# A two-layer transformer block on one core: the tiles that TensorE reads, all at one remainder of 512 bytes

## The chip, the core and the metric

The kernel runs on one core of a Trainium2 chip. A core has a matrix engine (TensorE, PE in the profile; PEld is its loading of weights), a vector engine (DVE), an activation engine (ACT), a general engine (POOL), an engine that issues transfers (SP), and 16 DMA engines. SBUF is the working memory, 128 partitions wide; PSUM takes the results of the matrix engine. The metric is the device time of one execution in microseconds (us).

A matmul on TensorE has two operands in SBUF. The *stationary* one, here up to 128 x 128 numbers, is loaded ahead as weights, by an instruction of its own. The *moving* one is then streamed through, here up to 512 columns. While one matmul streams its moving operand, the weights of the next are loaded, so there are two reads of SBUF at a time.

## The reference

`x` is 512 x 1024 in float32. Two layers, each of them:

```python
x = layer_norm(ALPHA * x + 0.5 * swiglu(x, ffn1_w1, ffn1_w2))   # (silu(x @ w1a) * (x @ w1b)) @ w2, width 2816
x = layer_norm(ALPHA * x + token_mix(x))
x = layer_norm(ALPHA * x + 0.5 * swiglu(x, ffn2_w1, ffn2_w2))
```

`token_mix` projects `x` with `w_in` (3616 columns) and runs three attentions side by side, each with 8 heads of 64: one over compressed, selected and windowed keys (`Nsa`), one over a window of 128 with sinks (`Swa`), and one with forget gates (`Fox`). Each result passes through a matrix of its own and a sigmoid gate of `x`, the three are added and multiplied with `w_out`.

## The kernel before, in words

**Numbers.** Every float32 matrix product of the dense parts is made of three products of rounded parts: a value is split into `hi` (rounded) and `lo` (the rest), and `hi*hi + lo*hi + hi*lo` is summed in PSUM. So nearly all matmuls come in threes. `xh` and `xl` hold the transposed input of a stage split in this way, 1024 x 512. Weights arrive by DMA as `raw` tiles of 512 KB; ACT makes `hi` of them (L140) and DVE makes `lo` (L141), in `wsplit` (L129).

**Two kinds of product.** In `mm3` (L155, matmuls L161 to L163; L158 and L159 for a narrow one) the weights are stationary and `xh`/`xl` move, 512 columns. In `mm_rows` (L169, matmuls L174 to L176) the activations are stationary, 128 columns at a time, and the weights `hi`/`lo` move, 512 columns. `value_rows` (L335, matmuls L345 to L347) does the latter with `xh`/`xl` as the stationary part.

**A feed-forward** (`ffn`, L271). `staged` (L255) computes the first four column blocks in halves of 256 moving columns, while the last tiles of the stage before are being transposed into `xh`/`xl` (`LN.second`, L211, transposes at L218). Then for f = 2 to 21 the gate block `pg` and the up block `pu` are computed, 24 matmuls each; their product goes as two rounded parts into `ha` (f below 18) and `hb` (the last 4). `rows_ln` (L223) then multiplies with `w2`: the main part runs over the 18 blocks of `ha`, 24 matmuls for each, into 8 accumulators `acc`; the last four, from `hb`, are done one row block at a time, so that each row block's layer norm (`LN.first`, L191) can start while PE goes on with the next. Before these last four, `ha`'s place is released and the pool `nx` is opened on it, into which the first weights of the next stage are loaded.

**The layer norm** of a row block: DVE adds the residual `xa` (L198), ACT squares (L201), POOL takes the power -1/2 in two small steps (L203, L204), DVE scales and shifts (L202, L207). The sums and the scale of a row are kept in `st`, 8 numbers a partition, one tile for each of the four row blocks.

**The mix** (`mix`, L352). `value_rows` first, from weights in `nx`. Then projections are cut into small pieces (`chunk`, three matmuls for a piece `pj`) which `step` (L995) puts between the attention's scores (`sS`, `sF`, `sN`, `sC`), transposes of the probabilities (`ptS`, `ptF`, `ptN`, `ptC`, against the identity `ident`) and products with the values (`po`). Afterwards the gates (`gate`), the three branch matrices (`brp`, with `oh`/`ol` moving) and `w_out` (`acc` from `mh`/`ml`) follow, and a layer norm.

**What sets the order.** The order on PE and POOL, and on SP at the beginning, is the order of the code; on the other engines a scheduler orders the instructions at build time.

**Where tiles lie.** SBUF is given out by pools. A pool opened later lies above (with `side="right"`, below the top), and within a pool tiles follow each other. Sizes in bytes per partition, addresses counted from the partition's beginning, before the change:

| tiles | pool | first address | remainder of 512 |
|---|---|---|---|
| `ident` | `const` | 16,512 | 128 |
| `xh`, `xl` | `xtp` | 19,776 | 320 |
| `raw`, `hi`, `lo` | `wt` (some `hi`, `lo` in `wx`, 89,408) | 52,544 | 320 |
| `hb`, and in the mix `mh`, `ml` | `fb`, `tl` | 105,792 | 320 |
| `st`, 4 x 32 bytes | `lnp` | 138,560 | |
| `ha`, 73,728 bytes | `fa` | 138,688 | 448 |
| `hi`, `lo` of a next stage | `nx` | 138,688 | 448 |
| `v4`, then `gt` of 384 bytes | `at` | 89,408 | 320 |
| `ks`, `qs`, `vt`, `p`, `pc` and others of the attention | `at` | 97,984 | 192 |
| `kc2`, `vbd` | `at` | 195,392 | 320 |
| `oh`, `ol` | `ohp` | 146,752 | 320 |
| `xa`, four residual tiles | `xap` | 212,960 | 480 |

`at.tile` without a tag gives a tile its place at its first call; `kc2` and `vbd` are first asked for in `conv2` (L575), after the small tiles of the first attention. `need` (L977) holds an `Nsa` unit back until `kc2` and `vbd` exist on `m`.

Of the kernel before, what the change touches and what calls it, by code (L numbers as in the profile page):

```python
# [9 lines left out]
F32 = mybir.dt.float32  # L10
F32R = mybir.dt.float32r
# [7 lines left out]
P = 128  # L19
S, D, F = 512, 1024, 2816  # L20
KD, KF, NB = D // P, F // P, S // P
H, DH, NSLOT = 8, 64, 32
# [42 lines left out]
def body(tc, a, out, depth=DEPTH):  # L65
# [3 lines left out]
    def pool(name, bufs=1, side=None, **kw):  # L69
        return tc.alloc_tile_pool(name=name, bufs=bufs, side=side, **kw)  # L70

    const = pool("const")
# [8 lines left out]
    def ps(tag=None, name="ps", shape=(P, 512)):  # L81
        if tag is None:
            tag = PS_ALL[ring[0] % 8]
            ring[0] += 1
        return psp.tile(list(shape), F32, name=name, tag=tag, bufs=PS_TAGS[tag])
# [15 lines left out]
    foxb = const.tile([P, depth, H], F32, name="foxb")  # L101
    bgate = const.tile([P, depth, 3, KD], F32, name="bgate")
    peT = const.tile([P, depth, 2, 32], F32, name="peT")

    xh = xtp.tile([P, KD, S], F32R, name="xh")
    xl = xtp.tile([P, KD, S], F32R, name="xl")
# [48 lines left out]
    def mm3(o, w, k, vh, vl, first, last):  # L155
        hi, lo = w
        if lo is None:
            nc.tensor.matmul(o[0:64], hi[:, k, 0:64], vh, start=first, stop=False)  # L158
            nc.tensor.matmul(o[0:64], hi[:, k, 0:64], vl, start=False, stop=last)  # L159
            return  # L160
        nc.tensor.matmul(o, hi[:, k], vh, start=first, stop=False)  # L161
        nc.tensor.matmul(o, hi[:, k], vl, start=False, stop=False)  # L162
        nc.tensor.matmul(o, lo[:, k], vh, start=False, stop=last)  # L163
# [15 lines left out]
    class LN:  # L179
# [10 lines left out]

        def first(self, acc, tb, tpl):  # L191
            x = self.xa[tb]
            st = self.pl.tile([P, 8], F32, name="st", bufs=4)
            junk = tpl.tile([P, D], BF, name="junk", bufs=2)
            u = tpl.tile([P, D], F32, name="u", bufs=2)
            hs = [slice(0, 512), slice(512, 1024)]
            for hf, c in enumerate(hs):
                nc.vector.scalar_tensor_tensor(x[:, c], acc[hf], self.scale, x[:, c], op0=OP.mult, op1=OP.add,  # L198
                                               accum_out=st[:, hf:hf + 1])
            nc.vector.tensor_scalar(st[:, 2:3], st[:, 0:1], st[:, 1:2], -1.0 / D, op0=OP.add, op1=OP.mult)  # L200
            nc.scalar.activation(junk, x, AF.Square, bias=st[:, 2:3], accum_out=st[:, 3:4])  # L201
            nc.vector.scalar_tensor_tensor(u, x, st[:, 2:3], self.G, op0=OP.add, op1=OP.mult)  # L202
            nc.gpsimd.tensor_scalar(st[:, 4:5], st[:, 3:4], 1.0 / D, EPS / ALPHA ** 2, op0=OP.mult, op1=OP.add)  # L203
            nc.gpsimd.tensor_tensor(st[:, 5:6], st[:, 4:5], mhalf, op=OP.pow)  # L204
            for c in hs:
                y = u if self.last else x
                nc.vector.scalar_tensor_tensor(y[:, c], u[:, c], st[:, 5:6], self.B[:, c], op0=OP.mult, op1=OP.add)  # L207
                if self.last:
                    nc.sync.dma_start(out[tb * P:(tb + 1) * P, c], y[:, c])
# [38 lines left out]

    def alloc_xa():
        p = pool("xap", side="right", reuse_waits="tile")  # L250
        return p, [p.tile([P, D], F32, name=f"xa{t}") for t in range(NB)]

    halves = [slice(0, 256), slice(256, 512)]

# [13 lines left out]
    def ffn_first(w1):  # L268
        return [wcols(w1, c) for c in (0, F, P, F + P)]
# [82 lines left out]
    def mix(l, wts, pend, done_ffn, xap, xa, nxt):  # L352
        m = K()
# [13 lines left out]
        at = pool("at", reuse_waits="tile")  # L367
# [1 line left out]
        for tb in range(NB):  # L369
            nc.scalar.activation(v4[:, tb], pts[tb], AF.Copy)  # L370
        m.vb, m.vs, m.vw = (v4[:, :, j] for j in range(3))
        gt = at.tile([P, NB, 24], F32, name="gt")
        tabs = {}

        def toep(i, mm):
# [198 lines left out]

        def conv2(c):  # L575

            m.kc2 = at.tile([P, 2, 2, NSLOT], F32R, name="kc2")
            m.vbd = at.tile([P, 2, P], F32, name="vbd")
            nc.gpsimd.memset(m.vbd, 0.0)
            p = ps("tp", "kv", (P, 3, 64))  # L580
            for f in range(2):
                nc.tensor.matmul(p[:, 0], c.wk[:, f].rearrange("p r d -> p (r d)"), c.gk[:, f], start=f == 0, stop=f == 1)
            for g in range(2):
                for f in range(2):
                    nc.tensor.matmul(p[0:64, 1 + g], c.gv[:, f, g].rearrange("p r n -> p (r n)"), c.wv[:, f],
                                     start=f == 0, stop=f == 1)
            hi, lo = m.kc2[:, :, 0], m.kc2[:, :, 1]
            pk = p[:, 0].rearrange("p (g n) -> p g n", g=2)
            nc.scalar.activation(hi, pk, AF.Copy, scale=0.5)
            nc.vector.scalar_tensor_tensor(lo, pk, 0.5, hi.bitcast(F32), op0=OP.mult, op1=OP.subtract)  # L590
            for r in range(2):
                o = slice(32 * r, 32 * r + 32)
                nc.scalar.activation(m.vbd[o, :, 64 * r:64 * r + 64], p[o, 1:3], AF.Copy, scale=0.5)
# [357 lines left out]
        fill.append(tr)  # L951
        chunk(CQA, set_q(m.qa, 0))
        fill.insert(len(fill) - 2, lambda: conv2(cv))
        fox_chunks(1)
        chunk(CQA + P, set_q(m.qa, 1))
# [21 lines left out]
        def need(u):  # L977
            if u.br == 1:
                return u.m in m.qb and hasattr(m, "kb")
            if u.br == 2:  # L980
                return u.m in m.qc and u.m in m.kc and u.m in m.vc and u.m in m.nck
            return u.m in m.qa and hasattr(m, "vbd") and hasattr(m, "kc2")

        batches = []
        for i in range(4):
# [9 lines left out]
        def step(cur, prev, n):  # L995


            for u in cur:
                while not need(u):
                    pump(1)  # L1000
                    n -= 1
# [85 lines left out]
        for d in range(KD):  # L1087
            g_t = gates0 if d == 0 else g_1 if d == 1 else gates(d)
            for br in (1, 2, 0):
# [3 lines left out]
                p = ps(name="brp")  # L1093
                for k in range(4):
                    mm3(p, w, k0 + k, oh[br][k], ol[br][k], k == 0, k == 3)
                t = g_t[br]
# [5 lines left out]
        ohp.release()  # L1102
        op.release()
        xap2, xa2 = alloc_xa()
        lnp = pool("lnp2", reuse_waits="tile")
        ln = LN(lnp, 1, l, xa2, 0.5)
# [12 lines left out]

    more_open()  # L1120
    xap, xa = alloc_xa()
    first_w = a["ffn1_w1"][0]
    pre = []
# [84 lines left out]
    for l in range(depth):  # L1208
        fin = l == depth - 1
        wts, pend, done = ffn(l, a["ffn1_w1"][l], a["ffn1_w2"][l], 0, xa, wts, pend, done, False, lambda: mix_first(l))  # L1210
        wts, pend, done, xap, xa = mix(l, wts, pend, done, xap, xa, lambda: ffn_first(a["ffn2_w1"][l]))
        wts, pend, done = ffn(l, a["ffn2_w1"][l], a["ffn2_w2"][l], 2, xa, wts, pend, done, fin,
                              lambda: None if fin else ffn_first(a["ffn1_w1"][l + 1]))
# [30 lines left out]
```

## Time and profile before

| | us |
|---|---|
| median of 3 runs | 2569.75 (2567.87 to 2570.13) |
| profiled execution, its own time | 2569.09 |
| its span, first to last instruction | 2567.4 |
| first feed-forward: `pg`/`pu`, from 41.3; `ha`, from 260.7 | |
| first mix: `vr` from 384.9, attention from 429.9, gates and branches from 709.6, `w_out` from 878.4 | |
| second feed-forward: `pg` from 948.3, `ha` from 1165.9 | |
| third feed-forward: `pg` from 1315.0, `ha` from 1532.7 | |
| second mix: `vr` from 1656.8 | |
| fourth feed-forward: `pg` from 2219.8, `ha` from 2437.4 | |

The granted TensorE clock was 0.998 of full speed over the span. In the rows of the profile, `L174 PE MATMUL acc<-hi,ha 128*128 128x512 f32 x576 | 227.3, 395 | 0.0` reads: line, engine, operation, result from moving and stationary tile, stationary size, moving size, count, then busy us in total, mean ns of one, and the engine's idle us just before. In a view of one tile the numbers after the count are shortest, median and longest duration in ns, then the first and the last start in us. In a timeline the first number is the start in us and the second the duration. Durations of matmuls overlap: the next starts before the last has ended.

### The profile page before, as it was taken

To read this page: it belongs to the slowest core of one execution; us is meant where nothing else is said; L and a number is where in the kernel's file an instruction comes from. 1 tells how busy PE (TensorE), PEld (TensorE's weight loads), DVE (VectorE), ACT (ScalarE), POOL (GpSimd) and SP (SyncE) were. 2 spreads that over 40 slices of the span, in tenths; PEclk is the share of its full clock that TensorE was granted. 3 is DMA by queue.
4 is the path that set the end of the run, shared out by engine and by line. 5 is a ranking of instruction groups with operands and counts; after the bars stand their busy time and mean duration, and the time that the engine had idled before them with its cause. 6 is when DMAs were issued, how large, how long until landed. Compare 5 with 4: busy or idle time off the path is not lost.

```text
span 2567.4 us, 34066 instructions
## 1 busy us (share of the span) xinstructions
PE 2545.5 (99%) x13099; PEld 2110.8 (82%) x13099; DVE 1214.1 (47%) x2617; ACT 927.4 (36%) x1895; POOL 187.6 (7%) x371
## 2 busy tenths in 40 slices
PE   9999999999999999999999999999999999999998
PEld 8888887788888888888888888877888888888887
DVE  4433245577654363332344432555776534544323
ACT  3222133476642332222232221345766323322211
POOL 0000000133300000000000000101332000000000
PEclk9999999999999999999999999999999999999999
DMA  6333234623143333333433333435321434233331
GB/s 213 111 98 99 95 96 122 181 79 83 50 140 102 120 100 98 99 99 91 115 91 94 95 98 99 116 117 155 95 75 42 146 101 148 81 93 98 99 94 63
DMA packets 375172, 268.98 MB, mean 105 GB/s; under 512 B 17385, under 2 KB 351273, under 8 KB 375009
## 3 DMA queue, kind: packets, MB, share of 16 engines
q1 hardware_dynamic: 373856, 262.61, 35.1%
q0 software_dynamic: 1152, 4.19, 0.4%
q8 instruction: 103, 1.69, 0.3%
q14 instruction: 61, 0.49, 0.1%
HBM read 247.83 MB, written 9.49 MB: 100 GB/s over the span
## 4 chain that ended last, share of the span: by engine, by line
PE 97%; DVE 1%; ACT 1%; DMA 1%; issue 0%; POOL 0%; DVEq 0%; POOLq 0%; SPq 0%; ACTq 0%
PE acc L176 7%; PE acc L174 7%; PE acc L175 7%; PE pg L161 6%; PE pg L162 6%; PE pg L163 6%; PE pu L161 6%; PE pu L163 6%; PE pu L162 6%; PE pj L161 5%; PE pj L163 5%; PE pj L162 5%; PE gate L161 3%; PE gate L162 3%; PE gate L163 3%; PE brp L162 2%
## 5 line engine op out<-in xcount | busy, mean ns | idle before, releaser
L141 DVE TENSOR_TENSOR lo<-raw,hi 128x1024 fp32r<-128x1024 f32 (+2 forms) x414 | 490.3, 1188 | 852.0 <-ACT hi L140 851.3
L140 ACT ACTIVATE hi<-raw 128x1024 fp32r<-128x1024 f32 (+2 forms) x414 | 424.4, 1031 | 1236.0 <-issue 702.2
L161 PE MATMUL pj<-xh,hi 128*128 128x512 f32 (+1 forms) x720 | 267.1, 371 | 1.5 <-ACT vt L448 1.4
L163 PE MATMUL pj<-xh,lo 128*128 128x512 f32 (+1 forms) x720 | 255.0, 354 | 0.2 <-DVE lo L141 0.2
L162 PE MATMUL pj<-xl,hi 128*128 128x512 f32 (+1 forms) x720 | 254.6, 354 | 0.0
L161 PE MATMUL pg<-xh,hi 128*128 128x512 f32 x640 | 249.9, 390 | 0.0
L162 PE MATMUL pg<-xl,hi 128*128 128x512 f32 x640 | 249.7, 390 | 0.0
L163 PE MATMUL pg<-xh,lo 128*128 128x512 f32 x640 | 249.5, 390 | 0.0
L163 PE MATMUL pu<-xh,lo 128*128 128x512 f32 x640 | 249.0, 389 | 0.0
L161 PE MATMUL pu<-xh,hi 128*128 128x512 f32 x640 | 249.0, 389 | 0.0
L162 PE MATMUL pu<-xl,hi 128*128 128x512 f32 x640 | 249.0, 389 | 0.0
L174 PE MATMUL acc<-hi,ha 128*128 128x512 f32 x576 | 227.3, 395 | 0.0
L175 PE MATMUL acc<-hi,ha 128*128 128x512 f32 x576 | 227.3, 395 | 0.0
L176 PE MATMUL acc<-lo,ha 128*128 128x512 f32 x576 | 227.2, 395 | 0.0
L286 DVE TENSOR_TENSOR t<-t,pu 128x512 f32<-128x512 f32 x80 | 55.0, 687 | 216.6 <-PE pu L163 216.6
L163 PEld LDWEIGHTS pj<-xh,lo 128*128 128x128 f32 x720 | 135.8, 189 | 20.1 <-DVE lo L141 0.4
L161 PEld LDWEIGHTS pj<-xh,hi 128*128 128x128 f32 x720 | 136.3, 189 | 17.6 <-issue 3.1
L203 POOL TENSOR_SCALAR st<-st 128x1 f32<-128x1 f32 x24 | 8.5, 355 | 1891.8 <-ACT junk L201 1891.8
L162 PEld LDWEIGHTS pj<-xl,hi 128*128 128x128 f32 x720 | 136.5, 190 | 11.4
L163 PEld LDWEIGHTS pg<-xh,lo 128*128 128x128 f32 x640 | 120.5, 188 | 25.2
L161 PEld LDWEIGHTS pg<-xh,hi 128*128 128x128 f32 x640 | 120.6, 188 | 25.0
L162 PEld LDWEIGHTS pg<-xl,hi 128*128 128x128 f32 x640 | 120.6, 188 | 24.8
(245 smaller groups left out, 4323.6 us busy)
## 6 DMA issues: line engine op xcount, KB each, us to landing
raw<-in_ffn_w_dram SPq DMA_DIRECT2D x264, 512.0 KB, 3.8
raw<-in_w_in_dram SPq DMA_DIRECT2D x56, 512.0 KB, 3.8
raw<-in_w_gate_dram SPq DMA_DIRECT2D x48, 512.0 KB, 4.2
ks<-hl SPq DMA_DIRECT2D x96, 128.0 KB, 2.4
raw<-in_w_out_dram SPq DMA_DIRECT2D x16, 512.0 KB, 3.6
tab<-bvec SPq DMA_DIRECT2D x16, 256.0 KB, 3.9
x_sp<-xa POOLq DMA_DIRECT2D x8, 512.0 KB, 6.7
cw<-in_cmp_k_w_dram SPq DMA_DIRECT2D x32, 128.0 KB, 3.5
```

What stands on the lines that cost most here:

```text
L140: nc.scalar.activation(hi[:, c], raw[:, c], AF.Copy)
L141: nc.vector.tensor_tensor(lo[:, c], raw[:, c], hi[:, c].bitcast(F32), op=OP.subtract)
L161: nc.tensor.matmul(o, hi[:, k], vh, start=first, stop=False)
L162: nc.tensor.matmul(o, hi[:, k], vl, start=False, stop=False)
L163: nc.tensor.matmul(o, lo[:, k], vh, start=False, stop=last)
L174: nc.tensor.matmul(o, sh(k)[:, t], hi[:, c], start=k == 0, stop=False)
L175: nc.tensor.matmul(o, sl(k)[:, t], hi[:, c], start=False, stop=False)
L176: nc.tensor.matmul(o, sh(k)[:, t], lo[:, c], start=False, stop=k == nk - 1)
L203: nc.gpsimd.tensor_scalar(st[:, 4:5], st[:, 3:4], 1.0 / D, EPS / ALPHA ** 2, op0=OP.mult, op1=OP.add)
L286: nc.vector.tensor_tensor(t, t, pu, op=OP.mult)
```

## The change

The four `st` tiles become `stats` in the pool `const`, with a `pad` of 48 numbers behind them (4 x 32 + 192 = 320 bytes), so that `xh` and all that follows starts at remainder 128, as `ident` does, and no small tile stands between `lnp` and `ha` or `nx`. All layer norms now share these four tiles. `xa` gets a pad of 88 numbers (352 bytes) above it and moves to 128 too. `gt` is 512 bytes instead of 384, of which 384 are used. `kc2` and `vbd` get their place right behind `gt`; since they then exist from the beginning of the mix, `need` looks at a new mark, `m.c2`, which `conv2` sets. After it every tile that TensorE reads, moving or stationary, starts at remainder 128 of 512.

```diff
@@ body
     peT = const.tile([P, depth, 2, 32], F32, name="peT")
+    stats = [const.tile([P, 8], F32, name=f"st{i}") for i in range(NB)]
+    const.tile([P, 48], F32, name="pad")
@@ LN.first
-            st = self.pl.tile([P, 8], F32, name="st", bufs=4)
+            st = stats[tb]
@@ alloc_xa
-        return p, [p.tile([P, D], F32, name=f"xa{t}") for t in range(NB)]
+        xa = [p.tile([P, D], F32, name=f"xa{t}") for t in range(NB)]
+        p.tile([P, 88], F32, name="pad")
+        return p, xa
@@ mix
-        gt = at.tile([P, NB, 24], F32, name="gt")
+        gt = at.tile([P, NB, 32], F32, name="gt")[:, :, 0:24]
+        m.kc2 = at.tile([P, 2, 2, NSLOT], F32R, name="kc2")
+        m.vbd = at.tile([P, 2, P], F32, name="vbd")
@@ conv2
-            m.kc2 = at.tile([P, 2, 2, NSLOT], F32R, name="kc2")
-            m.vbd = at.tile([P, 2, P], F32, name="vbd")
             nc.gpsimd.memset(m.vbd, 0.0)
...
+            m.c2 = True
@@ need
-            return u.m in m.qa and hasattr(m, "vbd") and hasattr(m, "kc2")
+            return u.m in m.qa and hasattr(m, "c2")
```

## The prediction

> **What bounds the kernel now.** I read the engine totals and the chain first.
>
> ```profile
> PE 2545.5 (99%) x13099; PEld 2110.8 (82%) x13099; DVE 1214.1 (47%) x2617; ACT 927.4 (36%) x1895; POOL 187.6 (7%) x371
> ...
> PE 97%; DVE 1%; ACT 1%; DMA 1%; issue 0%; POOL 0%; DVEq 0%; POOLq 0%; SPq 0%; ACTq 0%
> ```
>
> TensorE (PE) is busy in 99% of the span and holds 97% of the chain. So the time is the number of matmuls times the spacing of their starts, and only two things can shorten it: fewer matmuls or a closer spacing. A matmul's duration is no spacing, because neighbours overlap, but a change in duration hints at one. The groups kept apart by shape, all with 512 moving columns:
>
> ```profile
> L161 PE MATMUL pg<-xh,hi 128*128 128x512 f32 x640 | 249.9, 390 | 0.0
> ...
> L174 PE MATMUL acc<-hi,ha 128*128 128x512 f32 x576 | 227.3, 395 | 0.0
> ...
> L161 PE MATMUL brp<-oh,hi 128*128 128x512 f32 x192 | 74.7, 389 | 0.0
> ...
> L175 PE MATMUL acc<-hi,hb 128*128 128x512 f32 x128 | 49.8, 389 | 0.0
> ...
> L346 PE MATMUL vr<-hi,xl 128*128 128x512 f32 x64 | 25.2, 394 | 0.0
> ```
>
> The same shape takes 389 to 390 ns in one set of groups and 394 to 395 ns in another. The spacing comes from first and last starts in the tile views of `ha` and `pu` (inside the first feed-forward) and, for `hb`, from the timeline:
>
> ```profile
> L174 PE MATMUL acc<-hi,ha x144: 390/393/404, 260.7 to 360.4; 128*128 128x512 f32 x144
> L176 PE MATMUL acc<-lo,ha x144: 390/393/404, 261.2 to 360.9; 128*128 128x512 f32 x144
>   ACT hi L140: 72.2, 16
> ...
> L161 PE MATMUL pu<-xh,hi x160: 389/389/389, 48.6 to 260.1; 128*128 128x512 f32 x160
> L163 PE MATMUL pu<-xh,lo x160: 389/389/396, 49.0 to 260.5; 128*128 128x512 f32 x160
> ...
> 362.75 0.39 PE L175 MATMUL acc<-hi,hb 128*128 128x512 f32 x1
> ...
> 366.83 0.39 PE L175 MATMUL acc<-hi,hb 128*128 128x512 f32 x1
> ```
>
> `ha`: 3 x 144 = 432 matmuls, 431 steps from 260.7 to 360.9 us, 232.5 ns a step. `pu` alternates with `pg` in blocks of 24: 20 x 48 - 24 = 936 matmuls, 935 steps from 48.6 to 260.5, 226.6 ns. `hb`: 18 steps in 4.08 us, 226.7 ns. So `ha` pays 5.8 ns a matmul. `hb` and `ha` run the same three lines with the same kind of moving tile; they differ only in where the stationary tile lies. The third `ha` row is from the list of who waited: ACT waited 72.2 us, in 16 waits, for these matmuls, so the weights are ready ahead of PE and a faster PE finds them.
>
> Where do the tiles lie? Tiles of a pool follow each other in SBUF, in bytes per partition. `xh`, `xl`, the pool of `hi`/`lo`, `hb`, `mh`, `ml` and `oh`/`ol` start at remainder 320 of 512. The four statistics tiles of the layer norm (32 bytes each) stand in the pool below `ha`, and push `ha` and the pool `nx` to 448. The slow groups are those in which a moving row at one remainder is read while the next weights are loaded from the other: `ha` (moving 320, stationary 448) and `vr` (448, 320). Each fast group has one remainder for both. Address height is no explanation: `oh` moves from bytes 146,752 to 195,904, as high as `ha`, at 389 ns.
>
> **The change part by part.** It changes no arithmetic, no instruction count on PE and no order: on all five engines the instructions stand in the same order before and after (only `gt` is written as 4 x 24 instead of 96 elements). What changes is addresses, and then waits that go with addresses.
>
> (a) `ha` gets remainder 128 like all others: 4 feed-forwards x 432 = 1728 matmuls x 5.8 ns = 10.0 us off. All of it lies on PE, so all is span.
>
> (b) `vr`: 64 x 3 = 192 matmuls. Their durations are `ha`'s (394), so I take 5.7 ns: 1.1 us off.
>
> (c) The token mix. There the attention tiles stand at 192 (`gt` of 384 bytes pushed them), the identity at 128 and the projections at 320.
>
> ```profile
> L161 PE MATMUL pj<-xh,hi 128*128 128x512 f32 x464 | 193.8, 418 | 1.4 <-ACT vt L448 1.4
> L163 PE MATMUL pj<-xh,lo 128*128 128x512 f32 x464 | 182.3, 393 | 0.0
> L162 PE MATMUL pj<-xl,hi 128*128 128x512 f32 x464 | 181.9, 392 | 0.0
> ...
> 599.80 0.39 PE L161 MATMUL pj<-xh,hi 128*128 128x512 f32 x1
> 600.04 0.40 PE L162 MATMUL pj<-xl,hi 128*128 128x512 f32 x1
> 600.27 0.40 PE L163 MATMUL pj<-xh,lo 128*128 128x512 f32 x1
> 600.51 0.39 PE L807 MATMUL ptN<-ident,p 128*128 128x128 f32 x2
> ...
> 601.43 0.39 PE L161 MATMUL pj<-xh,hi 128*128 128x512 f32 x1
> 601.65 0.39 PE L162 MATMUL pj<-xl,hi 128*128 128x512 f32 x1
> ```
>
> At 600.27 a projection matmul runs while the weights of a transpose (`p`, other remainder) load: 240 ns to the next start, against 220 to 230 where projections follow each other (601.43 to 601.65). But 599.80 to 600.04 is 240 ns too, and there both remainders are equal: the projection has just followed attention work, and what it loses then need not be a matter of remainders. L162 never stands next to an attention weight and still has 392 ns. So the bounds are 0 and the whole excess over 389: (393 - 389) + (392 - 389) ns x 464 = 3.2 us on two lines, and some 5 us with a like share for L161 (an estimate from the same rows). I take 1.2 us off, about two thirds of L163's 4 ns x 464 = 1.9 us, because only that line is followed by weights at another remainder.
>
> (d) Matmuls with 256 moving columns (`staged`). Here the trace speaks against the change:
>
> ```profile
> 32.37 0.28 PE L163 MATMUL pj<-xh,lo 128*128 128x256 f32 x1
> ...
> 34.77 0.28 PE L162 MATMUL pj<-xl,hi 128*128 128x256 f32 x1
> ...
> 937.72 0.28 PE L162 MATMUL pj<-xl,hi 128*128 128x256 f32 x1
> ...
> 940.34 0.28 PE L163 MATMUL pj<-xh,lo 128*128 128x256 f32 x1
> ```
>
> In the first stage both tiles are at 320: 20 steps in 2.40 us, 120.0 ns. At 937 the weights come from `nx` at 448: 22 steps in 2.62 us, 119.1 ns. Equal remainders cost 0.9 ns here. Three stages move over: 3 x 192 = 576 matmuls, 0.5 us on.
>
> (e) Short matmuls of the mix.
>
> ```profile
> L807 PE MATMUL ptN<-ident,p 128*128 128x128 f32 x320 | 48.2, 273 | 3.9 <-DVE pc L393 3.0 <-ACT p L395 0.9
> L826 PE MATMUL po<-p,v 128*64 128x128 f32 x640 | 40.4, 273 | 0.0
> ```
>
> Transposes and the products with V have never had equal remainders, so there is no row. With the kinds left out here (L218, L706, L655, L713, L663, L820) they are some 2,100 records. Nearest is (d), also with a short stream: +0.9 ns at one end, and the same 0.9 ns as a gain at the other, so 1.9 us either way. I take 0.6 us on, nearer to the cost because (d) is the nearest row.
>
> (f) Waits. Moved addresses change which earlier tile's readers a new tile waits for; all of these are readers of an earlier stage, long done. Two edits leave a wait where none was: the statistics tiles are now shared by all layer norms, so POOL's write at L204 waits for DVE's reads of the layer norm before, and `kc2` and `vbd` get space at the beginning of the mix. The former stands in the tail of the program:
>
> ```profile
> 2559.35 0.39 PE L176 MATMUL acc<-lo,hb 128*128 128x512 f32 x1
> ...
> 2562.15 0.19 POOL L203 TENSOR_SCALAR st<-st 128x1 f32<-128x1 f32 x1 [4.62 <-ACT junk L201]
> 2562.42 0.55 POOL L204 TENSOR_TENSOR st<-st,mhalf 128x1 f32<-128x1 f32 x1
> ```
>
> The DVE reads waited for are those of the layer norm before, a whole feed-forward earlier, so the wait is met on arrival. Behind it in POOL's queue stands nothing, but DVE's L207 and the last store wait for its result. Bound: 0 to one more small POOL step, 0.2 us. I take 0. `kc2`, `vbd`: 0, because their old neighbours were read for the last time a stage earlier.
>
> Sum: -10.0 - 1.1 - 1.2 + 0.5 + 0.6 = -11.2 us. From the profiled execution's own 2569.09 us that gives 2557.9. That execution lies 0.7 us under the median shown, 2569.75; I say **2558**.
>
> **The rivals.**
>
> *Nothing changes* (2569). The two reads do not disturb each other, and the 5.8 ns come from something else that `ha` and `vr` share, for instance that their upper tiles lie in the pools opened last, at byte 138,688 and above. For it: only three remainders and few pairs occur. Against it: `oh` is as high and fast, and in `vr` the high tile moves while in `ha` it is stationary. The Trainium skill's page "SBUF — State Buffer", in its sections "SBUF: two separate sides" and "A bandwidth-pool intuition that's wrong (but worth ruling out)", speaks for this rival: TensorE has ports of its own and waits on nobody, and a second, independent read port serves weight loads. By that page nothing is to be had and the sum is 0; the trace's 232.5 beside 226.7 ns for one shape does not agree with two reads that never touch.
>
> *Slower: 128 is not 320.* All clean equal pairs of the trace are at 320. Should the remainder itself count, with 128 a bad one for streams of 512, every such matmul pays d ns over 226.7. Those equal now are `pg`, `pu`, `gate`, `brp`, `hb`, `mh`/`ml` and `pj`, 7,488; with `ha` and `vr` 9,408. Change: 9,408 x d - 1,920 x 5.7 ns, which is slower by over 5 us from d = 1.7 ns; at `ha`'s full 5.7 it is +42.7, 2612 us. For it: no pair at 128 has been seen. Against it: both mixed pairs, 320/448 and 448/320, cost the same, so the difference decides.
>
> *The mix gives more* (2553). If the whole 5 us of (c) go and (e) is a gain of 1.9 rather than a cost: -10.0 - 1.1 - 5 + 0.5 - 1.9 = -17.5, so 2552. For it: L161 and L162 are as slow as L163. Against it: equal remainders at 599.80.
>
> **How the numbers follow.** Forecast 0.74, the mix gives more 0.13, nothing 0.08, slower 0.05. The forecast's own range comes from its bounds: (c) 0 to 3.2, (e) -1.9 to 1.9, (f) up to 0.2, and 0.4 on (a) from rounded starts: 2554 to 2562. To take in the third rival and the spread of the runs shown (2567.87 to 2570.13) I go to **2551 to 2563**; outside stay the other two rivals and some of the edges. A measurement can tell 0.2%, 5 us, from no change. Faster 0.87, same 0.08, slower 0.05.
>
> **What would show it.** `ha` and `vr` at 389 ns and 226.7 ns a step, the `ha` stage 97.7 us from first to last start instead of 100.2; `pg`, `gate`, `brp`, `hb` unchanged; `pj` 256 wide at 120.0 in all four stages; L163 of `pj` nearer to 389, L162 where it is; transposes within 1 ns of now. I am wrong if `ha` stays at 395 (first rival), if `pg` rises over 390 (second), or if PE shows new idle time ahead of L161 or L807.

## The result and the profile after

The changed kernel takes 2557.57 us (median of 6 runs, 2555.65 to 2558.76), the kernel before beside it 2568.41. The ratio is 0.9956, 95% interval 0.9943 to 0.9969: 10.8 us or 0.4% less. The forecast was 2558 us, in a range of 2551 to 2563. The profiled execution has a span of 2557.0 us. The code has two more lines ahead of the matmuls, so L161 to L163 are now L163 to L165, and L174 to L176 are L176 to L178.

The engine totals of the changed kernel, and its groups by shape (busy us, mean ns of one, idle before):

```profile
PE 2534.7 (99%) x13099; PEld 2109.9 (83%) x13099; DVE 1215.6 (48%) x2617; ACT 927.3 (36%) x1895; POOL 188.3 (7%) x371
```

```profile
L163 PE MATMUL pg<-xh,hi 128*128 128x512 f32 x640 | 249.9, 390 | 0.0
...
L176 PE MATMUL acc<-hi,ha 128*128 128x512 f32 x576 | 224.1, 389 | 0.0
...
L163 PE MATMUL pj<-xh,hi 128*128 128x512 f32 x464 | 193.7, 417 | 1.4 <-ACT vt L454 1.4
L165 PE MATMUL pj<-xh,lo 128*128 128x512 f32 x464 | 182.1, 392 | 0.0
L164 PE MATMUL pj<-xl,hi 128*128 128x512 f32 x464 | 181.8, 392 | 0.0
L163 PE MATMUL brp<-oh,hi 128*128 128x512 f32 x192 | 74.7, 389 | 0.0
...
L164 PE MATMUL pj<-xl,hi 128*128 128x256 f32 x256 | 73.0, 285 | 0.6 <-DVE xl L223 0.6
...
L177 PE MATMUL acc<-hi,hb 128*128 128x512 f32 x128 | 49.8, 389 | 0.0
L812 PE MATMUL ptN<-ident,p 128*128 128x128 f32 x320 | 48.1, 273 | 4.0 <-DVE pc L399 3.0 <-ACT p L401 1.0
L831 PE MATMUL po<-p,v 128*64 128x128 f32 x640 | 40.4, 273 | 0.0
...
L350 PE MATMUL vr<-hi,xl 128*128 128x512 f32 x64 | 24.9, 389 | 0.0
```

PE's busy time fell by 10.8 us, as much as the median, at the same count of matmuls; the two profiled spans differ by 10.4 us. `ha` went from 395 to 389 ns and `vr` from 394 to 389; `pg`, `brp`, `hb`, the transposes and `po` stand where they stood, to 1 ns. The spacing, from the view of the tile `ha` in the first feed-forward and of `vr` in the first mix (shortest, median, longest ns, first and last start), for `vr` first the rows of the kernel before, which the prediction did not show, then those after:

```profile
L176 PE MATMUL acc<-hi,ha x144: 389/389/389, 260.7 to 358.0; 128*128 128x512 f32 x144
...
L178 PE MATMUL acc<-lo,ha x144: 389/389/389, 261.2 to 358.4; 128*128 128x512 f32 x144
...
  ACT hi L142: 70.0, 16
```

```profile
L345 PE MATMUL vr<-hi,xh x32: 390/393/481, 384.9 to 408.3; 128*128 128x512 f32 x32
...
L347 PE MATMUL vr<-lo,xh x32: 390/393/404, 385.4 to 408.7; 128*128 128x512 f32 x32
```

```profile
L349 PE MATMUL vr<-hi,xh x32: 389/389/476, 382.5 to 405.4; 128*128 128x512 f32 x32
...
L351 PE MATMUL vr<-lo,xh x32: 389/389/398, 383.0 to 405.9; 128*128 128x512 f32 x32
```

`ha`: 97.7 us over 431 steps, 226.7 ns, where it was 100.2 us. `vr` takes 23.4 us from first to last start instead of 23.8 (transposes stand between, so this is no spacing). ACT still waits for PE, 70.0 us in 16 waits, so the faster PE did not run into its weights.

### The profile page after: what moved, and what is told of

It reads as the page before. It is cut to its first block, busy times and chain, and to the rows that moved or that the text cites. A ratio compares the mean times of both kernels' runs of the same rounds, so it can differ in the third digit from the quotient of the medians.

```text
span 2557.0 us, 34082 instructions
## 1 busy us (share of the span) xinstructions
PE 2534.7 (99%) x13099; PEld 2109.9 (83%) x13099; DVE 1215.6 (48%) x2617; ACT 927.3 (36%) x1895; POOL 188.3 (7%) x371
## 4 chain that ended last, share of the span: by engine, by line
PE 95%; DVE 2%; DMA 1%; ACT 1%; issue 1%; POOL 0%; DVEq 0%; POOLq 0%; ACTq 0%
PE acc L176 7%; PE acc L178 7%; PE acc L177 7%; PE pg L163 6%; PE pg L164 6%; PE pg L165 6%; PE pu L164 6%; PE pu L163 6%; PE pu L165 6%; PE pj L163 5%; PE pj L165 5%; PE pj L164 5%; PE gate L163 3%; PE gate L165 3%; PE gate L164 3%; PE brp L163 2%
## 5 line engine op out<-in xcount | busy, mean ns | idle before, releaser
L163 PE MATMUL pj<-xh,hi 128*128 128x512 f32 (+1 forms) x720 | 267.3, 371 | 1.5 <-ACT vt L454 1.4
L164 PE MATMUL pj<-xl,hi 128*128 128x512 f32 (+1 forms) x720 | 254.8, 354 | 0.6 <-DVE xl L223 0.6
L165 PE MATMUL pj<-xh,lo 128*128 128x512 f32 (+1 forms) x720 | 254.9, 354 | 0.1
L163 PE MATMUL pg<-xh,hi 128*128 128x512 f32 x640 | 249.9, 390 | 0.0
L164 PE MATMUL pg<-xl,hi 128*128 128x512 f32 x640 | 249.7, 390 | 0.0
L165 PE MATMUL pg<-xh,lo 128*128 128x512 f32 x640 | 249.5, 390 | 0.0
L163 PE MATMUL pu<-xh,hi 128*128 128x512 f32 x640 | 249.0, 389 | 0.0
L164 PE MATMUL pu<-xl,hi 128*128 128x512 f32 x640 | 249.0, 389 | 0.0
L165 PE MATMUL pu<-xh,lo 128*128 128x512 f32 x640 | 249.0, 389 | 0.0
L176 PE MATMUL acc<-hi,ha 128*128 128x512 f32 x576 | 224.1, 389 | 0.0
L177 PE MATMUL acc<-hi,ha 128*128 128x512 f32 x576 | 224.1, 389 | 0.0
L178 PE MATMUL acc<-lo,ha 128*128 128x512 f32 x576 | 224.1, 389 | 0.0
L165 PEld LDWEIGHTS pj<-xh,lo 128*128 128x128 f32 x720 | 136.4, 190 | 20.0 <-DVE lo L143 0.3
L163 PEld LDWEIGHTS pj<-xh,hi 128*128 128x128 f32 x720 | 136.8, 190 | 17.5 <-issue 3.1
L164 PEld LDWEIGHTS pj<-xl,hi 128*128 128x128 f32 x720 | 137.2, 190 | 12.3 <-DVE xl L223 0.9
L165 PEld LDWEIGHTS pg<-xh,lo 128*128 128x128 f32 x640 | 120.7, 189 | 25.4
L163 PEld LDWEIGHTS pg<-xh,hi 128*128 128x128 f32 x640 | 120.6, 188 | 25.0
L163 PEld LDWEIGHTS pu<-xh,hi 128*128 128x128 f32 x640 | 120.1, 188 | 25.2
```

The source lines that it names most:

```text
L176: nc.tensor.matmul(o, sh(k)[:, t], hi[:, c], start=k == 0, stop=False)
L177: nc.tensor.matmul(o, sl(k)[:, t], hi[:, c], start=False, stop=False)
L178: nc.tensor.matmul(o, sh(k)[:, t], lo[:, c], start=False, stop=k == nk - 1)
```

## The experiments

Twelve kernels were run. In the runs without an interval the reading is the spacing, and the time only a check. "Distance" is from now on the stationary tile's address less the moving one's, taken modulo 256, unless a larger number is given. Where an expectation says that the residual is at 480, the kernel also leaves out the pad behind the residual, which the edits below don't show; of the tiles that TensorE reads only the residual `xa` moves by it, in transposes that take 273 to 274 ns (L220) with the pad and without.

**One part alone.** The kernel before, and only a pad in each layer norm's pool:

```diff
@@ LN.__init__
+            pl.tile([P, 128 - 4 * 8], F32, name="pad")
```

> The kernel before, with nothing but 384 unused bytes beside the statistics tiles of each layer norm, so that ha and the tiles of nx lie at remainder 320 like hi, lo, xh and xl; the statistics tiles stay where they were, the attention stays at 192, the residual at 480. Theory (the gain is ha and vr at one remainder): ha at 226.7 ns a step and 389 ns a matmul, vr too, the time some 10.5 us under the kernel before, 2558. Rival (the gain needs the whole layout, or comes from the statistics tiles being shared): 2568, or a part of the way.

2557.69 us (5 runs), ratio to the kernel before 0.9954, interval 0.9940 to 0.9967. The view of `ha` in its first feed-forward, and its `vr` by shape:

```profile
L174 PE MATMUL acc<-hi,ha x144: 389/389/389, 259.3 to 356.5; 128*128 128x512 f32 x144
...
L176 PE MATMUL acc<-lo,ha x144: 389/389/389, 259.7 to 357.0; 128*128 128x512 f32 x144
```

```profile
L347 PE MATMUL vr<-hi,xl 128*128 128x512 f32 x64 | 24.9, 390 | 0.0
```

97.7 us for 431 steps, 226.7 ns. The whole gain is there, and neither the moved statistics tiles nor the attention's new places are in this kernel. That `ha` lies even 384 bytes higher than before also ends the rival of the high address.

**The attention alone undone.** The changed kernel with the old `gt`:

```diff
-        gt = at.tile([P, NB, 32], F32, name="gt")[:, :, 0:24]
+        gt = at.tile([P, NB, 24], F32, name="gt")
```

> The changed kernel with gt at 384 bytes again, so that kc2, vbd and all attention tiles (ks, qs, vt, p, pc) stand at remainder 0 while projections, values and identity stay at 128. Theory (in the mix only the one matmul ahead of an attention weight gains, about 200 of them by some 2 to 6 ns): 0.3 to 1.2 us more than the changed kernel, not to be told from it in the time; the last matmul ahead of attention work at 233 to 234 ns. Rival (the mix gives some 5 us): 2562.5.

2558.40 us, ratio 0.9956 (0.9943 to 0.9968), not to be told from the changed kernel. Its projections in the mix:

```profile
L165 PE MATMUL pj<-xh,lo 128*128 128x512 f32 x464 | 182.2, 393 | 0.0
L164 PE MATMUL pj<-xl,hi 128*128 128x512 f32 x464 | 182.0, 392 | 0.0
```

Against the changed kernel's 392 and 392 that is one ns on L165, and 0.1 and 0.2 us of busy time. The starts in the two traces show where it lies. Only 238 of the 464 L165 matmuls stand ahead of attention work; their steps are longer by 0.33 us in all, 1.4 ns each, and the other projections' by 0.05 us. The mix hardly gains, and L164 keeps its 392 with all remainders equal.

**All at 256.** The changed kernel with `pad` of 80 numbers behind the statistics tiles and 56 behind the residual:

> The changed kernel with 128 bytes more of padding behind the statistics tiles: everything TensorE reads lies at remainder 256, only the identity stays at 128. Theory (the difference decides, not the remainder, and transposes don't care): all matmuls of 512 columns at 226.7 ns a step, transposes as in the changed kernel, 2557.6. Rival (the remainder itself counts): pg, pu, gate, brp and ha at another spacing than 226.7, up to 2612 at 232.4. Rival (transposes with unequal remainders cost): some 850 of them by 1 to 6 ns, up to 5 us.

2554.64 us (4 runs), ratio 0.9943 (0.9929 to 0.9956); the interval overlaps the changed kernel's. By shape:

```profile
L163 PE MATMUL pg<-xh,hi 128*128 128x512 f32 x640 | 249.9, 390 | 0.0
...
L176 PE MATMUL acc<-hi,ha 128*128 128x512 f32 x576 | 224.1, 389 | 0.0
...
L812 PE MATMUL ptN<-ident,p 128*128 128x128 f32 x320 | 48.1, 273 | 3.9 <-DVE pc L399 3.0 <-ACT p L401 1.0
```

Every row with 512 columns is the changed kernel's to 1 ns, so the remainder itself does not count, and transposes do not mind an identity 128 bytes apart. What makes the 2.9 us between the medians is not shown; of the 1.9 us between the two profiled spans 1.3 lie in the steps of the matmuls with 256 columns, among them one wait of 0.6 us that the changed kernel's execution had.

**Which distances are clean.** Each kernel gives the four feed-forwards four distances, by a pad below `ha` or by an offset within it (shown with the first four numbers of each kind; the second kernel has the other four):

```diff
@@ LN.__init__, 32, 64, 128, 256 and 96, 160, 224, 288 bytes
+            if which != 1:
+                pl.tile([P, (32, 64, 128, 256)[2 * l + which // 2] // 4], F32, name="pad")
@@ ffn, 4, 16, 192, 64 and 8, 48, 240, 272 bytes
+        n, d = 2 * NA * S, (1, 4, 48, 16)[2 * l + which // 2]
+        st.ha = fa.tile([P, n + 64], F32R, name="ha")[:, d:d + n].rearrange("p (a k s) -> p a k s", a=2, k=NA)
```

> The changed kernel, its pad behind the residual taken away (residual at 480), with ha and nx moved up by 32, 64, 128 and 256 bytes in the first to the fourth feed-forward; all moving and other tiles stay at 128. Theory (only equal remainders of 512 are free, and any other distance costs the same): ha at about 232.4 ns a step in all four, the time at 2568. Rival (the period is 256): the fourth at 226.7. Rival (the cost grows with the distance): the first nearest to 226.7, the fourth the slowest.

> As the run before, with distances of 96, 160, 224 and 288 bytes. Theory (any distance costs the same): 232.4 ns a step in all four, 2568. Rival (the cost follows the distance): the spacings of these four lie between or beyond those at 64, 128 and 256 bytes in order.

> The changed kernel (residual at 480) with ha set off inside its tile by 4, 16, 192 and 64 bytes in the first to the fourth feed-forward. Theory (a few bytes are as bad as many): 231 to 235 ns a step in all four, some 2568. Rival (reads go by blocks, and only another block is unequal): 4 or 16 bytes at 226.7. 64 bytes gave 233.3 in the second feed-forward of an earlier run and should give the same in the fourth.

> As the run with 4, 16, 192 and 64 bytes, now with 8, 48, 240 and 272 bytes. If what repeats every 256 bytes repeats here, 272 is as clean as 16 was, 226.7 ns a step. If the sign does not matter, 240 (16 bytes short of 256) is clean too. If any odd multiple of 16 is clean, 48 and 240 are as well. 8 bytes: 231 to 235, as 4. The time from the spacings: 144 x 3 x 5.7 ns = 2.5 us for each slow feed-forward over the changed kernel.

The first of the three lines in the views of `ha`, one row for each feed-forward, kernel by kernel in this order:

```profile
L176 PE MATMUL acc<-hi,ha x144: 392/395/396, 259.3 to 359.3; 128*128 128x512 f32 x144
...
L176 PE MATMUL acc<-hi,ha x144: 393/396/398, 1164.7 to 1264.8; 128*128 128x512 f32 x144
...
L176 PE MATMUL acc<-hi,ha x144: 390/393/404, 1531.3 to 1631.0; 128*128 128x512 f32 x144
...
L176 PE MATMUL acc<-hi,ha x144: 389/389/389, 2436.8 to 2534.0; 128*128 128x512 f32 x144
```

```profile
L176 PE MATMUL acc<-hi,ha x144: 392/397/400, 260.6 to 361.1; 128*128 128x512 f32 x144
...
L176 PE MATMUL acc<-hi,ha x144: 394/394/394, 1166.3 to 1266.4; 128*128 128x512 f32 x144
...
L176 PE MATMUL acc<-hi,ha x144: 393/395/397, 1533.6 to 1633.7; 128*128 128x512 f32 x144
...
L176 PE MATMUL acc<-hi,ha x144: 392/395/396, 2438.8 to 2538.9; 128*128 128x512 f32 x144
```

```profile
L176 PE MATMUL acc<-hi,ha x144: 388/392/399, 259.2 to 358.9; 128*128 128x512 f32 x144
...
L176 PE MATMUL acc<-hi,ha x144: 389/389/389, 1163.6 to 1260.8; 128*128 128x512 f32 x144
...
L176 PE MATMUL acc<-hi,ha x144: 392/392/392, 1528.2 to 1626.4; 128*128 128x512 f32 x144
...
L176 PE MATMUL acc<-hi,ha x144: 393/396/398, 2431.1 to 2531.2; 128*128 128x512 f32 x144
```

```profile
L176 PE MATMUL acc<-hi,ha x144: 391/392/397, 257.6 to 356.5; 128*128 128x512 f32 x144
...
L176 PE MATMUL acc<-hi,ha x144: 396/396/397, 1161.7 to 1261.8; 128*128 128x512 f32 x144
...
L176 PE MATMUL acc<-hi,ha x144: 389/389/389, 1529.0 to 1626.2; 128*128 128x512 f32 x144
...
L176 PE MATMUL acc<-hi,ha x144: 389/389/389, 2430.7 to 2527.9; 128*128 128x512 f32 x144
```

From first to last start there are 143 x 3 = 429 steps in each row. Each distance but 64 was run in one feed-forward only. Which one it is makes no difference by itself: at one distance for all, the four take 232.3 to 232.5 ns a step before the change and 226.5 to 226.7 after. The mean step, in ns:

| bytes | 4 | 8 | 16 | 32 | 48 | 64 | 96 | 128 |
|---|---|---|---|---|---|---|---|---|
| step | 232.4 | 230.5 | 226.6 | 233.1 | 233.3 | 233.3 (twice) | 234.3 | 232.4 |

| bytes | 160 | 192 | 224 | 240 | 256 | 272 | 288 |
|---|---|---|---|---|---|---|---|
| step | 233.3 | 228.9 | 233.3 | 226.6 | 226.6 | 226.6 | 233.3 |

The theory that only equal remainders of 512 are clean fell: 256 is clean, and so are 16 bytes to either side of 256 and 16 above 0. The theory of a cost that grows with the distance fell too: 4 bytes cost as much as 128. Where two distances 256 bytes apart were run, they agree (16 and 272, 32 and 288). 192 alone lies between. The times, one run each, follow: 2565.98, 2570.93, 2563.22 and 2559.92 us.

**Which read meets which.** `ha` cut into its two parts, the one that is stationary for L177 alone 128 bytes off:

```diff
...
-        st.ha = fa.tile([P, 2, NA, S], F32R, name="ha")
+        ha = fa.tile([P, NA, S], F32R, name="ha")
+        fa.tile([P, 32], F32, name="pad")
+        st.ha = ha, fa.tile([P, NA, S], F32R, name="hl")
```

> The changed kernel (residual at 480) with the second part of ha, which is the stationary tile of L175 of the kernel before alone, 128 bytes off; the first part, stationary for L174 and L176, stays at 128 like the moving tiles. Theory (the moving read of one matmul meets the weight load of the next): the step from an L174 matmul to the next start, in which L175's weights load, at 232.4 ns, the other two at 226.7; 576 x 5.7 ns = 3.3 us on the changed kernel, 2561. Rival (a matmul is slow when its own two operands differ): the step after L175 is the slow one, at the same total. Rival (both reads spoil the neighbourhood): more than one of three slow, up to 2567.

2564.38 us (one run), between the theory's 2561 and the 2567 of the last rival. The views of its tiles `ha` and `hl` over all feed-forwards:

```profile
L176 PE MATMUL acc<-hi,ha x576: 396/396/396, 259.2 to 2532.4; 128*128 128x512 f32 x192
L178 PE MATMUL acc<-lo,ha x576: 389/389/389, 259.7 to 2532.8; 128*128 128x512 f32 x192
```

```profile
L177 PE MATMUL acc<-hi,hl x576: 397/397/397, 259.4 to 2532.6; 128*128 128x512 f32 x192
```

Two of three are slow: L176, in which the odd weights are loaded, and L177, whose own weights they are. So the theory held for half of what happened. L177 can be slow for itself, or because L176 left it disturbed. The next kernel takes these apart by shifting the `lo` weights of the pool `wt`, which *move* in L178 and are stationary in L165:

```diff
@@ wsplit, at its first call on wt
+            wt.tile([P, 32], F32, name="pada")
         lo = pl.tile([P, KD, P], F32R, name="lo", tag="lo", bufs=nb)
+            wt.tile([P, 32], F32, name="padb")
```

> The changed kernel (residual at 480) with the lo weights of the pool wt 128 bytes off; hi stays at 128, and ha, hb, the weights of wx and all later tiles move up by 256, a distance that cost nothing in the run with ha at 256. In the main part of rows_ln the lo weights move in the third matmul of three (L178 of the changed kernel): while it streams, weights at a clean distance are loaded that differ by 128 from what streams, and its own operands differ as well; the other two have nothing unequal. Theory A (a disturbed matmul leaves the next one disturbed, as after attention work in the mix): the step after the third and the step after the first matmul of the next three are both slow, 232 to 234 ns. Theory B (own operands and loaded weights count each for itself): only the step after the third is slow, the first stays at 226.7. Both: the products with moving xh and xl pay some 13 ns for three, where lo lies in wt, so that the time is near 2580.

2574.62 us (one run), 5 us under the 2580 that was expected; where these lie was not looked into. Its L182 to L184 are the changed kernel's L176 to L178, its L169 to L171 the changed kernel's L163 to L165. The views of `ha` and `gate`:

```profile
L182 PE MATMUL acc<-hi,ha x576: 388/388/389, 260.1 to 2542.5; 128*128 128x512 f32 x192
L183 PE MATMUL acc<-hi,ha x576: 389/389/389, 260.3 to 2542.7; 128*128 128x512 f32 x192
L184 PE MATMUL acc<-lo,ha x576: 389/395/395, 260.5 to 2542.9; 128*128 128x512 f32 x192
```

```profile
L169 PE MATMUL gate<-xh,hi x304: 389/389/499, 706.9 to 2145.2; 128*128 128x512 f32 x152
L170 PE MATMUL gate<-xl,hi x304: 393/396/396, 707.2 to 2145.4; 128*128 128x512 f32 x152
L171 PE MATMUL gate<-xh,lo x304: 395/397/397, 707.5 to 2145.7; 128*128 128x512 f32 x152
```

L182 follows a slow L184 and is as fast as ever, 388: a disturbed matmul does not leave the next one disturbed, and theory A fell. (L184 at 389 is the share, 232 of 576, whose moving `lo` lies in `wx`, at a clean distance.) With `lo` stationary, L170 is slow while it is loaded and L171 while it is used. So a matmul of 512 columns is slow when what it streams is at a bad distance from the weights being loaded, and also when it is at a bad distance from its own. Both at once cost no more: L184 at 395. Why its own should still count is open. In the kernel with `hl`, a load is on record from 300.11 us for 0.19 us and its matmul starts at 300.34, so the load looks finished; but if the load of badly placed weights in truth reached into the stream of its own matmul, one disturbance, between a load and whatever streams meanwhile, would explain both slow lines. No run here separates these two.

**Can bad distances pay?** The kernel with 64 bytes in its second feed-forward had shown a median step of 114 ns instead of 120 in the matmuls of 256 columns that follow it, whose weights lay 64 bytes off too. Three kernels put a pad ahead of the first weights in `nx` (the comment is added here):

```diff
@@ ffn_first
+        nx.pool.tile([P, 32], F32, name="pad")    # 128 bytes; 64 in the second; 32, 96, 192 in the third
```

> The changed kernel (residual at 480) with 128 bytes ahead of the weights that a feed-forward's first four column blocks use out of nx, so that the matmuls of 256 columns there have unequal remainders again, and all else equal ones. Theory (where the weight load sets the pace, unequal remainders save 0.9 ns): 576 x 0.9 = 0.5 us less than the changed kernel, 2557.1, which the time can't tell but the spacing can: 119.1 instead of 120.0 ns. Rival (that difference was another thing, such as bytes arriving): 120.0 ns.

> The changed kernel (residual at 480) with 64 bytes ahead of a feed-forward's first weights in nx, the distance at which matmuls of 256 columns had a median step of 114 ns in an earlier run. If that step holds in all three such stages: 576 x 4.4 ns (120.0 to 115.6 in the mean) = 2.5 us under the changed kernel, 2555.1. Rival (the stage waits for bytes or for the transposes in it, so that closer matmuls only wait longer): 2557.6 with the step at 115 and longer waits.

> The changed kernel (residual at 480) with 32, 96 and 192 bytes ahead of the first weights in nx in the three stages of 256 columns that read from there. If the step falls with any distance that is not a multiple of 128: 114 to 116 ns in all three. If 64 is a place of its own: 119 to 121 at 32 and 96. If the period is 256 and the sign does not matter: 192 as 64, 114.

128 bytes: 2557.35 us, ratio 0.9952 (0.9938 to 0.9965). 64 bytes: 2555.99 us (5 runs), ratio 0.9945 (0.9931 to 0.9959). The third: 2556.45, one run. The timeline of the kernel with 64 bytes, in the second and the fourth feed-forward's first blocks:

```profile
932.74 0.28 PE L164 MATMUL pj<-xl,hi 128*128 128x256 f32 x1
...
935.91 0.28 PE L165 MATMUL pj<-xh,lo 128*128 128x256 f32 x1
```

```profile
2195.74 0.28 PE L164 MATMUL pj<-xl,hi 128*128 128x256 f32 x1
...
2198.92 0.28 PE L164 MATMUL pj<-xl,hi 128*128 128x256 f32 x1
```

28 steps in 3.17 us, 113.2 ns, in the one, and 27 in 3.18 us, 117.8 ns, in the other, at the same distance by the code; why they differ is open. The kernel with 128 bytes, in its second feed-forward's first blocks:

```profile
931.75 0.28 PE L165 MATMUL pj<-xh,lo 128*128 128x256 f32 x1
...
936.97 0.28 PE L164 MATMUL pj<-xl,hi 128*128 128x256 f32 x1
```

44 steps in 5.22 us, 118.6 ns, where equal places give 120.0. Over the whole stage, with steps over 130 ns left out, the mean is 118.8 ns in the second and the fourth feed-forward and 119.7 in the third, against 119.8 in the changed kernel. So the theory of this kernel held in two stages of three, and unequal places are what gave the kernel before its 119 ns there.

Mean steps with small waits in them (the mean of the differences between neighbouring starts, waits over 260 ns left out) were 119.7 ns at 32 and at 96 bytes, 118.7 at 192, 120.0 at 128 and 116.9 at 64, against 120.9 in the same three stages of the changed kernel. So short streams do gain a little from a bad distance, most at 64. 576 x 4.0 ns would be 2.3 us; between the medians lie 1.6 us, and the two intervals overlap; the kernel with 64 bytes and the one at 256 have the lowest medians, and neither is shown to beat the changed kernel.

## Why the prediction was right

**The bound.** PE was and is busy for 99%, and the spacing showed in the span, which is 10.4 us shorter in the profiled execution. The 13,099 matmuls stand in the same order in both traces, so the steps from one start to the next can be subtracted one by one: (a) -9.9 us, (b) -1.0, (c) -0.4, (d) +1.3, (e) +0.3, all others -0.7.

**(a)** forecast 10.0 us. 100.2 - 97.7 = 2.5 us in each of four stages: 10.0, and 9.9 by the steps. Right, and shown by the pad alone.

**(b)** forecast 1.1. The steps became 1.0 us shorter, and durations fell from 394 to 389, as `ha`'s did. Right in kind and size.

**(c)** forecast 1.2, too much: it was 0.4 by the steps, 0.1, 0.1 and 0.2 us by the busy time of the three lines, and undoing the attention's part alone gave back as much. The step that failed is the size of the term: it took two thirds of L163's 4 ns for a matter of the weights behind it and counted them on all 464 matmuls. Only 238 of these stand ahead of attention work, and their steps fell by 1.4 ns each, 0.33 us. The mechanism is there, at a quarter of the size. The rest of the excess is on L162 too, which the change leaves, and stays with every remainder equal. What makes projections after attention work slow was not tried and stays open; that it is carried over from an unequal matmul is unlikely, since in the run with moving `lo` nothing was carried over.

**(d)** forecast 0.5 on, at 120.0 ns in all stages. In the second feed-forward's first blocks after the change:

```profile
935.84 0.28 PE L164 MATMUL pj<-xl,hi 128*128 128x256 f32 x1
...
938.60 0.28 PE L163 MATMUL pj<-xh,hi 128*128 128x256 f32 x1
```

23 steps in 2.76 us, 120.0 ns. Steps without a wait became longer by 0.2 us in each of the three stages, 0.6 in all, and the kernel with 128 bytes ahead of `nx` took this back in two of them. Right in kind and size. The other 0.7 us of the 1.3 are one wait in the second feed-forward's first blocks: PE idle for 0.6 us ahead of an L164, for DVE's `xl` (L223). The prediction had named no such wait, and it isn't in the profiled execution of the kernel with 128 bytes.

**(e)** forecast 0.6 on, taken between unknown ends. It was near 0: `ptN` at 273 and 273 ns, 48.2 and 48.1 us in total, `po` the same to the digit. Of the 0.3 us that the steps show, 0.2 lie on the 32 `ptC`, and 0.1 are spread over the other 2,064 matmuls. The nearest row, (d), was no guide for 128 columns.

**(f)** forecast 0. In the tail POOL's second step starts 0.27 us after the first, as before: at 2551.73 and 2552.00 us now, at 2562.15 and 2562.42 then. Right.

The misses of (c) and (d) lengthen the time by 0.8 us each, those of (e) and of the matmuls that the sum left out shorten it by 0.3 and 0.7; so most of it cancels, by luck. That 2558 lies 0.4 us from the median is luck, too, with runs of one kernel 3 us apart and the sum taken from a single execution; the forecast fall was 11.2 us, and it was 10.8 between the medians.

**The rivals.** *Nothing changes* fell with the pad alone. With it the rule of the Trainium skill's page "SBUF — State Buffer" (section "SBUF: two separate sides"), by which TensorE waits on nobody, does not hold here as far as its own two reads go: one and the same shape runs at 226.6 or 234.3 ns a step by the distance of two tiles, and the measurement decides. *128 is not 320* fell with `pg` at 390 at 128 and again at 256. *The mix gives more* fell with (c).

What the prediction had too narrow is the rule itself. It gave the period as 512, as the change does, and put the cost on the next weights alone. The runs put the period at 256, with clean places 16 bytes around it, and found the matmul that uses the weights to be slow as well. Neither touches the sum, because `ha` and `vr` were at 128 bytes in both senses.

## What to carry to other kernels

Where TensorE is busy throughout, compare the durations of one shape between groups: 395 beside 389 ns was 5.8 ns a step, and the cause was 128 bytes of small tiles ahead of a large one. Put the tiles that TensorE reads for streams of 512 columns at one remainder of 256 bytes, and keep small tiles out of the pools between them; here a pad of 384 bytes did what the whole change did. For streams of 256 and 128 columns, look first: here equal places cost the former about 1 ns a step and gained the latter nothing.

## What the runs showed of the hardware

A matmul with 512 float32 moving columns starts 226.6 ns after the one before, if its moving tile lies 0, 16, 240, 256 or 272 bytes from the stationary ones, and after 229 to 234 ns at 4, 8, 32, 48, 64, 96, 128, 160, 192, 224 or 288; a period of 256 bytes fits all of these. A distance of 4 bytes was as bad as 128, and 16 as good as 0; why is open. The cost falls on the matmul that streams while bad weights load (396 ns) and on the one that uses them (397), and not on the one after (389). With 256 moving columns the order turns: 120.0 ns when equal, 118.6 at 128 bytes, 113.2 or 117.8 at 64.
